# A hybrid encoder step on one Trainium2 core: the modulation of six token tiles made in two halves of the channels

## Chip, core and metric

The kernel runs on one core of one Trainium2 chip. The metric is the device time of one execution in microseconds (us), median over the runs. TensorE (PE in the profile) multiplies; VectorE (DVE), ScalarE (ACT) and GpSimd (POOL) do the rest; SyncE (SP) issues the transfers between HBM and the on-chip memory in one queue.

## What is computed

One layer of a streaming encoder, for a prompt of 2048 tokens and a decode tile of 64 tokens. Its start is what matters here:

```python
mod = jax.nn.silu(c) @ w_ada + b_ada                  # c: (1, 1024), w_ada: (1024, 3072)
shift, scale, gate = jnp.split(mod, 3, axis=-1)
h = _rmsnorm(x, norm_g) * (1.0 + scale[:, None, :]) + shift[:, None, :]
proj = h @ w_in                                       # w_in: (1024, 3080)
u, z_s, q, k, v, z_a, f_logit = jnp.split(proj, IN_SPLITS, axis=-1)
...                                                   # state-space branch on u, attention on q, k, v
y = x + gate[:, None, :] * (mixed @ w_out)
```

u has 512 columns and feeds the state-space branch; f_logit has 8. Everything is float32.

## The kernel before

**Tiles.** The prompt is cut into four groups of 512 tokens, a group into four tiles of 128 tokens (two pairs), the 1024 channels into eight tiles k of 128. Group 3 has the decode tile as well. Pair (g, i) means tiles i and i+1 of group g. float32 products are made as three products of rounded halves: hi x hi, hi x lo, lo x hi, so each weight and each h exists as a `hi` and a `lo` tile (in the profile `whi`, `wlo`, and two tiles that are both named `h`).

**Modulation (class Ada).** The prompt's and the sample's c are transposed and passed through silu into `cT`. `chunk(n)` (n from 0 to 5) loads 512 columns of `w_ada` as two DMAs of 1 MB (tile `wada`, L361), multiplies them with `cT` (eight matmuls per half, four at a time in separate rows of the array), copies the sums to `ms` (ACT, L371), transposes `ms` (four transposes, L127) and reduces them to columns in `mt` (L376). Chunk 0 gives the shift of channel tiles 0 to 3 (`shf`, L388), chunk 1 that of tiles 4 to 7; chunks 2 and 3 give the same for the scale (`gsc`, L390 and L391); 4 and 5 give the gate. A `wada` tile has 16 KB per partition and there are four.

**h (class InProj).** `load(g, i0)` brings in a pair's two x tiles of 0.5 MB (L429), takes the sum of squares (ACT Square, L432), 1/sqrt (`rsq`, L289 on DVE, L290 on POOL) and scales x (DVE, L434). There are four x buffers. `norm(g)` goes through the pairs of a group and, for each two channel tiles, transposes the scaled x (TensorE, L127, two banks), applies scale and shift in the copy out of PSUM (ACT, `hf`, L459) and splits `hf` into hi and lo (DVE, L280 and L284). `put(g)` stores h of groups 0 and 1 to HBM (L469) for the later columns.

**The u columns.** `weights` loads 256 columns of w_in (8 more for f_logit where u's part 0 is meant) as two halves of 0.5 MB (`wst`, L484) and splits each into `whi` (ACT, L282) and `wlo` (DVE, L284). `natural("u", part, groups)` makes, for each token tile, 24 matmuls (8 k, three products; L124, 264 columns in part 0, 256 in part 1) into a PSUM bank, copies it out (L523) and stores it (L538).

**Order.** The program is written as a sequence and a scheduler orders the instructions of each engine; a transfer is issued in the order of the SP queue, and each issue waits for one of eight completion counters, taken in turn. The start is written so: x of pair (0,0); the first w_in weights (u part 0); chunks 0, 2, 1, 3; `params()` (three small loads, L244 to L246); h of groups 0 and 1 and their stores; u parts 0 and 1 of these groups; chunks 4 and 5; `masks()` (a swap matrix and six masks, by selects on POOL and copies on DVE, L252 to L264); then groups 2 and 3.

## Time and profile before

| | us |
|---|---|
| median of three runs | 1456.5 |
| lowest, highest | 1455.73, 1466.12 |
| the profiled execution | 1460.03 |
| its span in the trace | 1458.3 |
| PE busy | 1374.8 (94%) |
| DVE busy | 909.4 (62%) |
| ACT busy | 541.5 (37%) |
| POOL busy | 480.5 (33%) |

The span is the time between the first and the last instruction of the profiled execution. Busy times are sums over the whole span; what bounds the kernel in one stage has to be read from that stage. PE's busy time counts matmuls, PEld the loading of the stationary operand, which runs beside them. A row of a timeline stands for a run of equal instructions: its start, the time from the first to the last of them, and in brackets how long the engine had been idle before and what ended that. The profiled execution is 3.5 us longer than the median run.

### The profile page before, as it was taken

Reading aid. Unit: us, or ns where it says so; the run is one execution under the profiler, and the core shown is the slowest. Engines: PE = TensorE matmul, PEld = TensorE weight load, DVE = VectorE, ACT = ScalarE, POOL = GpSimd, SP = SyncE. Lnnn points to the kernel's source line nnn. Section 1 sums busy time; section 2 is a strip of 40 time slices with the busy share of each in tenths; the row PEclk is TensorE's granted clock in tenths of the full one; section 3 lists DMA queues with packets and bytes.
Section 4 is the critical chain, followed back from the end, with each engine's and each line's share of the span. In section 5 each row is a group of like instructions: output and inputs, shape, how many; then the busy total and the mean of one; then the engine's idle time right before and its main releaser. Section 6 shows DMA issues by size and latency. Waiting matters only on the chain. (4 is left out here: it accounts for less than half of the span.)

```text
span 1458.3 us, 26193 instructions
## 1 busy us (share of the span) xinstructions
PE 1374.8 (94%) x9730; PEld 1082.7 (74%) x9730; DVE 909.4 (62%) x2406; ACT 541.5 (37%) x1156; POOL 480.5 (33%) x452
## 2 busy tenths in 40 slices
PE   5899989999999999999999999999999897999998
PEld 2798889889888889998878855555555454478887
DVE  2646898678767795564214777886886877342331
ACT  3755215343433444333324435445445344300000
POOL 1101356235322362231125413423324527322222
PEclk9999999999999999999999989999999999999999
DMA  9875423323335725235458623133121222054452
GB/s 336 297 274 150 120 65 85 103 81 89 114 88 165 259 77 139 67 98 148 132 169 252 183 93 107 45 98 93 55 74 38 87 63 91 23 159 147 136 150 94
DMA packets 209383, 184.01 MB, mean 126 GB/s; under 512 B 66823, under 2 KB 169955, under 8 KB 208232
## 3 DMA queue, kind: packets, MB, share of 16 engines
q1 hardware_dynamic: 209256, 182.35, 40.8%
q8 instruction: 76, 1.25, 0.4%
q14 instruction: 51, 0.42, 0.1%
HBM read 125.16 MB, written 57.15 MB: 125 GB/s over the span
## 5 line engine op out<-in xcount | busy, mean ns | idle before, releaser
L124 PE MATMUL low<-whi,h 128*128 128x256 f32 (+1 forms) x2112 | 406.9, 289 | 12.7 <-DVE ev L534 7.3
L124 PEld LDWEIGHTS low<-whi,h 128*128 128x128 f32 x2112 | 337.4, 193 | 23.2 <-issue 11.9
L124 PE MATMUL low<-wlo,h 128*128 128x256 f32 (+1 forms) x1088 | 307.9, 286 | 0.6 <-DVE wlo L284 0.6
L1220 DVE CUSTOM_DVE_ANT_0 pb<-twin,cb 128x512 bf16<-128x512 f32 (+3 forms) x328 | 199.7, 609 | 62.8 <-PE twin L124 51.4
L124 PEld LDWEIGHTS low<-wlo,h 128*128 128x128 f32 x1088 | 209.2, 192 | 2.2 <-issue 1.2
L304 ACT ACTIVATE p<-twin 128x1024 f32<-128x1024 f32 (+3 forms) x180 | 150.0, 839 | 146.1 <-PE twin L124 137.4
L124 PE MATMUL low<-h,whi 128*128 128x512 f32 (+1 forms) x640 | 176.7, 362 | 0.0
L124 PE MATMUL bank<-p,vt 128*64 128x512 f32 (+3 forms) x704 | 143.6, 530 | 0.0
L124 PE MATMUL twin<-qs,ks 64*128 64x512 f32 (+3 forms) x1056 | 134.2, 359 | 0.0
L124 PEld LDWEIGHTS low<-h,whi 128*128 128x128 f32 x640 | 115.0, 192 | 17.7 <-issue 1.7
L290 POOL TENSOR_TENSOR qss<-qss,mhalf 128x4 f32<-128x4 f32 (+1 forms) x68 | 77.2, 1137 | 143.0 <-DVE qss L289 118.9
L124 PE MATMUL low<-h,wlo 128*128 128x512 f32 (+1 forms) x320 | 115.4, 361 | 0.0
L284 DVE TENSOR_TENSOR wlo<-wst,whi 128x512 fp32r<-128x512 f32 (+1 forms) x96 | 67.8, 718 | 76.2 <-ACT whi L282 73.5
L1297 DVE TENSOR_TENSOR acc<-acc,p 128x1024 f32<-128x1024 f32 (+4 forms) x89 | 87.5, 983 | 28.7 <-ACT p L304 27.1
L124 PEld LDWEIGHTS twin<-qs,ks 64*128 64x128 f32 x1056 | 95.2, 191 | 10.9
L124 PE MATMUL twin<-sm,kb 64*128 64x512 f32 (+3 forms) x360 | 78.0, 428 | 17.5 <-DVE pm L1220 17.0
L124 PEld LDWEIGHTS bank<-p,vt 128*64 128x64 f32 x704 | 45.4, 141 | 65.6 <-issue 56.2
L175 POOL TENSOR_TENSOR yo<-yo,x 128x512 f32<-128x512 f32 (+1 forms) x34 | 49.0, 1441 | 133.6 <-DVE yo L1531 133.6
L124 PE MATMUL last<-oh,mh 128*128 128x512 f32 (+1 forms) x208 | 81.4, 391 | 0.0
L124 PE MATMUL last<-ol,mh 128*128 128x512 f32 (+1 forms) x208 | 81.1, 390 | 0.0
L124 PE MATMUL last<-oh,ml 128*128 128x512 f32 (+1 forms) x208 | 81.1, 391 | 0.0
L124 PEld LDWEIGHTS twin<-sm,kb 64*128 64x128 f32 x360 | 34.6, 188 | 60.4 <-DVE pm L1220 40.0
(365 smaller groups left out, 2503.8 us busy)
## 6 DMA issues: line engine op xcount, KB each, us to landing
wst<-in_w_in_dram SPq DMA_DIRECT2D x48, 512.0 KB
h<-h SPq DMA_DIRECT2D x16, 1024.0 KB
wada<-in_w_ada_dram SPq DMA_DIRECT2D x12, 1024.0 KB
cb<-cb_d SPq DMA_DIRECT2D x20, 512.0 KB
x<-in_x_prompt_dram SPq DMA_DIRECT2D x16, 512.0 KB
out_dram<-ev SPq DMA_DIRECT2D x64, 128.0 KB
x<-in_x_prompt_dram SPq DMA_DIRECT2D x32, 256.0 KB
out_dram<-yo SPq DMA_DIRECT2D x32, 256.0 KB
```

What stands on the lines that cost most here:

```text
L124: return self.keep(self.pe.matmul(*a, **kw))
L175: PL.tensor_tensor(out, x, y, op=op)
L284: V.tensor_tensor(lo, x, hi, op=ALU.subtract)
L290: PL.tensor_tensor(out, out, bc(mhalf[:out.shape[0]], list(out.shape)), op=ALU.pow)
L304: i = S.activation(out, x, func, **kw)
L1220: V.tensor_tensor_reduce(b[:, :n], ps[:, h, :n], cb[:, h, :n], 1.0, NEG, ALU.add, ALU.max, accum_out=self.pm[:, t, h, pi:pi + 1])
L1297: (PL if j else V).tensor_tensor(y[:rows, :, c0:nq], x[:rows, :, c0:nq], p[:rows, :, :n], op=ALU.add)
```

## The change

A new method `begin` takes the place of the first steps. It makes the h of three pairs, (0,0), (0,2) and (1,0), and multiplies it with u part 1 (columns 256 to 511), in two halves of the channels. Three PSUM banks are held for it, one per pair; each holds the sums of two tiles. For k = 0 to 3, which need chunks 0 and 2 only, each pair is transposed, scaled, split and multiplied (24 matmuls of 256 columns) into its bank; then chunks 1 and 3 are computed, and k = 4 to 7 are added to the same banks. After that the sums are copied out and stored, h of pair (1,2) is made, u part 1 of its two tiles follows, and u part 0 of both groups comes behind that.

The loads of the start have an order of their own, which is pinned on the SP queue: chunks 0 and 2, the first half of w_in's columns (k 0 to 3), x of (0,2), chunk 1, x of (1,0), chunk 3, the second half of w_in's columns. For this `Ada.load` is a method apart from `chunk`, with a tile of 8 KB per partition for each half (four such tiles), `norm` is cut into `normal(g, i0, ks)` and `weights` into `half(k0, c0, n)`. x has six buffers instead of four.

```diff
+    @contextmanager
+    def ordered(*engines):
+        start = len(nc.cur_bb.bb.instructions)
+        yield
+        last = {}
+        for i in nc.cur_bb.bb.instructions[start:]:
+            if not engines or i.engine in engines:
+                if i.engine in last:
+                    tc.add_manual_dep(i, last[i.engine], nosync)
+                last[i.engine] = i.name
...
-        self.wp = Region(e.nc, (R_S5K[0], R_S5U[1] - 4), (18, 36), (54, 72), bufs=4)
+        self.wp = Region(e.nc, (R_S5K[0], R_S5K[0] + 32), bufs=4)
...
+    def load(self, n):
+        for k2 in range(2):
+            w = self.wp.tile([P, 4, 512], F32, name="wada")
+            self.e.nc.sync.dma_start(w, self.e.w_ada[512 * k2:512 * k2 + 512, n * 512:n * 512 + 512]
+                                     .rearrange("(k p) c -> p k c", p=P))
+            self.w[n, k2] = w
...
-        self.xp = Region(e.nc, R_X, (R_S5U[1] - 4, R_S5U[1]))
+        self.xp = Region(e.nc, R_X, (R_S5U[1] - 4, R_S5U[1]), (R_S5K[0] + 32, R_S5K[0] + 40))
...
-            x = self.xp.tile([P, D], F32, tag="x", name="x", bufs=4)
+            x = self.xp.tile([P, D], F32, tag="x", name="x", bufs=6)
...
+    def normal(self, g, i0, ks):
...
+        xs = self.normed[g, i0]
+        c0 = P * i0
+        w = sum(r for _, r in xs)
+        for k in ks:
+            pt = self.pst.tile([P, 2, 256], F32, tag="tr", name="tr")
...
+    def half(self, k0, c0, n):
...
+        st = self.wp.tile([P, 4, 264], F32, tag="wst", name="wst", bufs=2)
+        off = 0
+        for c, w in zip(c0, n):
+            e.nc.sync.dma_start(st[:, :, off:off + w], e.w_in[P * k0:P * k0 + 512, c:c + w].rearrange("(k p) c -> p k c", p=P))
+            off += w
...
+    def begin(self, ad):
+        e = self.e
+        nc, S, PE = e.nc, e.S, e.PE
+        pairs = [(0, 0), (0, 2), (1, 0)]
+        with e.ordered(nc.sync.engine):
+            ad.load(0)
+            ad.load(2)
+            w = [self.half(0, [256], [256])]
+            self.load(0, 2)
+            for n in (0, 2):
+                ad.chunk(n)
+            ad.load(1)
+            self.load(1, 0)
+            ad.load(3)
+            w.append(self.half(4, [256], [256]))
+        banks = [self.ps.hold() for _ in pairs]
+        for n in range(2):
+            if n:
+                for i in (1, 3):
+                    ad.chunk(i)
+            for (g, i0), pm in zip(pairs, banks):
+                self.normal(g, i0, range(4 * n, 4 * n + 4, 2))
+                hi, lo = self.h[g]
+                for j in range(2):
+                    cs = slice(P * (i0 + j), P * (i0 + j + 1))
+                    for k in range(4):
+                        kk = 4 * n + k
+                        for q, (x, y) in enumerate(((hi, 0), (hi, 1), (lo, 0))):
+                            PE.matmul(pm[:, 256 * j:256 * j + 256], x[:, kk, cs], w[n][y][k][:, :256], start=kk == q == j == 0,
+                                      stop=kk == KT - 1 and q == 2, skip_group_check=True)
+        for (g, i0), pm in zip(pairs, banks):
+            del self.normed[g, i0]
+            for j in range(2):
+                t = self.ev.tile([P, 256], F32, tag="ev", name="ev", bufs=4)
+                S.copy(t, pm[:, 256 * j:256 * j + 256])
+                t0 = 512 * g + P * (i0 + j)
+                nc.sync.dma_start(e.u_d[t0:t0 + P, 256:], t)
+            self.ps.free(pm)
+        self.normal(1, 2, range(0, KT, 2))
+        del self.normed[1, 2]
+        self.natural("u", 1, (1,), (w[0][0] + w[1][0], w[0][1] + w[1][1], 256), first=2)
...
         ip.load(0, 0)
         ad = Ada(e)
-        w = ip.weights([0, 3072], [256, 8])
-        for n in (0, 2, 1, 3):
-            ad.chunk(n)
+        ip.begin(ad)
         e.params()
-
         for g in range(2):
-            ip.norm(g)
             ip.put(g)
-        ip.natural("u", 0, (0, 1), w)
-        ip.natural("u", 1, (0, 1))
+        ip.natural("u", 0, (0, 1))
         for n in (4, 5):
+            ad.load(n)
             ad.chunk(n)
         e.masks()
```

The lines named above have other numbers after the change: w_ada is loaded in L371, x in L444, squared in L447 and scaled in L449, w_in is loaded in L512, `ms` copied in L386, `hf` made in L478, h stored in L488, u copied and stored in L558 and L560 for the first six tiles.

The scheduler's order, engine by engine, shows where the steps have gone. First SyncE's queue at the start. `DMAHW0` to `DMAHW7` are the eight completion counters: an issue that waits for one waits for the DMA eight issues before it. Before:

```order
L333 DMA brow_0_163<-in_b_ada_dram 1x1024
L484 DMA wst_0_203<-in_w_in_dram 128x4x256 [waits DMAHW0_49]
L484 DMA wst_0_203<-in_w_in_dram 128x4x8 [waits DMAHW1_49]
L484 DMA wst_1_214<-in_w_in_dram 128x4x256 [waits DMAHW2_49]
L484 DMA wst_1_214<-in_w_in_dram 128x4x8 [waits DMAHW3_49]
L361 DMA wada_0_225<-in_w_ada_dram 128x4x512 [waits DMAHW4_49]
L361 DMA wada_0_225<-in_w_ada_dram 128x4x512 [waits DMAHW5_49]
L361 DMA wada_1_244<-in_w_ada_dram 128x4x512 [waits DMAHW6_49]
```

After, from the first half of w_in's columns on (the four `wada` loads of chunks 0 and 2 stand directly ahead of it, behind `brow`):

```order
L512 DMA wst_0_211<-in_w_in_dram 128x4x256 [waits DMAHW4_49]
L444 DMA x_2_221<-in_x_prompt_dram 128x1024 [waits DMAHW5_49]
L444 DMA x_3_228<-in_x_prompt_dram 128x1024 [waits DMAHW6_49]
L244 DMA bfb_0_107<-in_b_f_dram 128x8 [waits DMAHW7_49]
L245 DMA kg_0_105<-in_k_norm_g_dram 128x64 [waits DMAHW0_49]
L246 DMA qg_0_106<-in_q_norm_g_dram 128x64 [waits DMAHW1_49]
L512 DMA wst_0_211<-in_w_in_dram 128x4x8 [waits DMAHW2_49]
L512 DMA wst_1_286<-in_w_in_dram 128x4x8 [waits DMAHW3_49]
L647 DMA cl_0_1460<-in_cache_logf_dram 128x4x8 [waits DMAHW4_49,DVE_49]
L371 DMA wada_0_203<-in_w_ada_dram 128x4x512 [waits DMAHW5_49,PE_49]
L371 DMA wada_1_205<-in_w_ada_dram 128x4x512 [waits DMAHW6_49,PE_49]
L444 DMA x_4_270<-in_x_prompt_dram 128x1024 [waits DMAHW7_49]
```

The modulation weights of chunks 0 and 2 now stand ahead of w_in; six small loads stand between x_3 and chunk 1, and chunk 1's first load waits for the landing of x_2 (DMAHW5) and for TensorE's use of the buffer.

Second, ScalarE around the copy of chunk 3's sums (`ms_1<-bank_73`). Before:

```order
L371 COPY ms_0_236<-bank_77 128x512
L371 COPY ms_1_255<-bank_73 128x512
L432 ACTIVATE sq_0_143,ss_2_343<-x_2_341 128x1024
L459 ACTIVATE hf_0_311<-low_120,shf_0_112,gsc_0_111 128x256 x2
L459 ACTIVATE hf_1_320<-low_124,shf_0_112,gsc_0_111 128x256 x2
```

After:

```order
L386 COPY ms_0_243<-bank_77 128x512
L478 ACTIVATE hf_0_302<-low_120,shf_0_112,gsc_0_111 128x256 x2
L478 ACTIVATE hf_1_311<-low_124,shf_0_112,gsc_0_111 128x256 x2
L282 CAST whi_2_288<-wst_1_286 128x2x256
L282 CAST whi_3_292<-wst_1_286 128x2x256
L386 COPY ms_1_259<-bank_73 128x512
L282 CAST whi_4_697<-wst_0_211 128x528
```

Between the copies of chunks 1 and 3 there are now scalings of a pair and the two casts of w_in's second half.

Third, VectorE where h of pair (1,2) begins (x_0 and x_1 are its two tiles). Before, the masks stand far behind, among the splits of the decode tile:

```order
L260 MEMSET msk_0_966 128x128
L463 COPY h_16384_1_391<-h_53248_1_392 128x2x64
L264 CAST m_qk_207360_0_93<-msk_0_966 128x128
L256 CAST identw_0_92<-swap_0_957 128x128
L260 MEMSET msk_0_966 128x128
L280 CAST h_16384_1_391<-hf_1_320 128x2x64
```

After:

```order
L449 TENSOR_SCALAR x_0_141<-x_0_141,ss_0_144 128x1024
L260 MEMSET msk_0_970 128x128
L289 TENSOR_SCALAR ss_1_151<-ss_1_151 128x1
L256 CAST identw_0_92<-swap_0_961 128x128
L264 CAST m_qk_207360_0_93<-msk_0_970 128x128
L260 MEMSET msk_0_970 128x128
L449 TENSOR_SCALAR x_1_149<-x_1_149,ss_1_151 128x1024
L264 CAST m_qk_207616_0_94<-msk_0_970 64x128
L260 MEMSET msk_0_970 128x128
L264 CAST m_qk_207616_0_94<-msk_0_970 64x128
L260 MEMSET msk_0_970 128x128
L264 CAST m_kq_207872_0_95<-msk_0_970 128x128
```

Four of the six masks now stand between the scaling of x_0 and the first split of that pair's h, which is two rows further on.

More of the change, by code (lines that the diff above doesn't have):

```diff
@@ L438, in norm @@
     def norm(self, g):
+        for i0 in range(0, len(self.tiles(g)), 2):
+            self.normal(g, i0, range(0, KT, 2))
+            del self.normed[g, i0]
+    def normal(self, g, i0, ks):
         e = self.e
@@ L493, in weights @@
-        return hi, lo, off
-    def natural(self, kind, part, gs, w=None):
+            h, l = self.half(k0, c0, n)
+            hi += h
+            lo += l
+        return hi, lo, sum(n)
+    def half(self, k0, c0, n):
+        e = self.e
+        hi, lo = [], []
+        st = self.wp.tile([P, 4, 264], F32, tag="wst", name="wst", bufs=2)
[3 more added lines that the diff above has]
+            off += w
+        for k in range(0, 4, 2):
+            h = self.wp.tile([P, 2, 264], F32R, tag="whi", name="whi", bufs=5)
+            l = self.wp.tile([P, 2, 264], F32R, tag="wlo", name="wlo", bufs=5)
+            e.split(st[:, k:k + 2, :off], h[:, :, :off], l[:, :, :off], el=self.wlo)
+            hi += [h[:, 0], h[:, 1]]
+            lo += [l[:, 0], l[:, 1]]
+        return hi, lo
@@ L497, in natural @@
+    def natural(self, kind, part, gs, w=None, first=0):
         e = self.e
@@ L505, in natural @@
             ts = self.tiles(g)
-            for i, (t0, r, s) in enumerate(ts):
+            for i, (t0, r, s) in list(enumerate(ts))[first:]:
                 pm = self.ps.tile([P, 512], F32, tag="mm", name="mm")
```

64 lines of the change are left out of this document (21 added, 43 removed).

## Prediction

> **What bounds the kernel now.** I read the busy time by stage first, the stages cut at two events: 39.17 us, when TensorE starts the first matmul that needs the second half of the channels, and 140.59 us, when it starts the first u matmul of token groups 2 and 3. Columns: length, then PE, PEld, DVE, ACT and POOL busy, granted TensorE clock, DMA share, GB/s.
>
> ```profile
> core 0: us, PE busy (x) PEld busy (x) DVE busy (x) ACT busy (x) POOL busy (x), PEclk, DMA share, GB/s
> 0.00:39.17 39.17, 20.95 (x122) 9.16 (x123) 11.73 (x42) 14.51 (x25) 4.68 (x22) 1.00 0.96 327
> 39.17:140.59 101.42, 95.93 (x737) 85.72 (x736) 61.23 (x154) 61.18 (x132) 10.89 (x23) 0.98 0.72 251
> 140.59:1458.30 1317.71, 1257.87 (x8876) 987.77 (x8873) 836.44 (x2212) 465.83 (x1000) 464.95 (x407) 0.98 0.37 111
> 14.90:34.00 19.10, 16.15 (x100) 6.75 (x104) 3.39 (x11) 3.69 (x7) 0.00 (x0) 1.00 1.06 387
> 60.00:70.00 10.00, 8.65 (x71) 8.19 (x70) 6.57 (x15) 8.01 (x17) 1.10 (x2) 1.00 0.92 334
> ```
>
> The last stage holds 1317.71 of 1458.30 us, and the change leaves its instructions as they are. All that can be gained lies in the first two: TensorE is idle there for 18.2 and 5.5 us. In the first the DMA engines are full (0.96; 387 GB/s while the modulation weights stream), so the bound is the order in which bytes come. In the second TensorE is the bound, and its waits are few:
>
> ```profile
> PE low L127 <- ACT hf L459: 6.0, 5, 2.3
> PE low L127 <- DVE x L434: 1.2, 1, 1.2
> PE low L127 <- DVE ss L289: 0.3, 1, 0.3
> ```
>
> That is 7.5 us; the one of 2.3 us ends at the border (it is the wait behind 38.88 below), so 5.2 us belong to the second stage. Last I read the timeline of the start, column by column: start, duration, engine and line, and in brackets what the engine had waited for.
>
> ```profile
> 0.81 0.88 SPq L429 DMA_DIRECT2D x<-in_x_prompt_dram  x2
> 4.39 1.06 ACT L432 ACTIVATE sq<-x 128x1024 bf16<-128x1024 f32 x1 [2.31 <-DMA x<-in_x_prompt_dram]
> 4.39 2.80 SPq L484 DMA_DIRECT2D wst<-in_w_in_dram  x4
> 11.84 1.17 ACT L282 CAST whi<-wst 128x528 fp32r<-128x528 f32 x2 [0.48 <-DMA wst<-in_w_in_dram]
> 14.90 1.94 PE L124 MATMUL bank<-wada,cT 128*32 128x512 f32 x8 [4.36 <-DMA wada<-in_w_ada_dram]
> 17.61 1.93 PE L124 MATMUL bank<-wada,cT 128*32 128x512 f32 x8 [0.77 <-DMA wada<-in_w_ada_dram]
> 23.03 0.20 PEld L124 LDWEIGHTS low<-wada,cT 128*32 128x32 f32 x8 [1.54 <-DMA wada<-in_w_ada_dram]
> 25.84 1.06 PE L124 MATMUL bank<-wada,cT 128*32 128x512 f32 x8
> 28.06 0.39 PE L124 MATMUL low<-whi,h 128*128 128x264 f32 x1
> 33.98 0.30 PEld L124 LDWEIGHTS bank<-wada,cT 128*32 128x32 f32 x8 [0.56 <-DMA wada<-in_w_ada_dram]
> 35.30 0.59 ACT L371 COPY ms<-bank 128x512 f32<-128x512 f32 x1 [4.35 <-PE bank L124]
> 35.94 0.66 PE L127 MATMUL bank<-ident,ms 128*128 128x128 f32 x4 [0.76 <-ACT ms L371]
> 38.88 0.30 PE L127 MATMUL low<-ident,x 128*128 128x128 f32 x1 [2.28 <-ACT hf L459]
> ```
>
> Read it as four facts. The halves of the modulation weights, 1 MB each, land 2.71 us apart (14.90 and 17.61; the fourth at 23.03, the eighth at 33.98). A 0.5 MB tile issued at 0.81 into an idle queue is there at 4.39: 1.36 us for its bytes and 2.2 us of latency. From the landing of the half that completes shift and scale of the first four channel tiles (23.03) to the first h matmul (28.06) pass 5.0 us. From the transposes of the last chunk (35.94) to the first matmul of the second half (39.17) pass 3.2 us.
>
> **The start, term by term.** The 1 MB of w_in that stood ahead goes behind. The first half is then issued when x_0 has landed, at 4.39, lands at 4.39 + 2.2 + 2.7 = 9.3, and the fourth, which completes chunks 0 and 2, at 17.4 where it was 23.03. The scales could be used 5.0 us later, at 22.4, but three things stand ahead of the first h matmul on TensorE and ScalarE: the casts of half the w_in weights, Square of x_2 and x_3, and their transposes. 1.5 MB after 17.4 put x_3 at 21.5. What a landed x tile still needs is seen here:
>
> ```profile
> 59.51 1.06 ACT L432 ACTIVATE sq<-x 128x1024 bf16<-128x1024 f32 x1 [2.59 <-DMA x<-in_x_prompt_dram]
> 62.31 0.87 PE L127 MATMUL low<-ident,x 128*128 128x128 f32 x6 [1.22 <-DVE x L434]
> 42.07 0.29 PE L124 MATMUL low<-whi,h 128*128 128x264 f32 x1
> 42.19 0.28 PE L124 MATMUL low<-wlo,h 128*128 128x264 f32 x1
> 42.31 0.28 PE L124 MATMUL low<-whi,h 128*128 128x264 f32 x1
> 46.90 0.60 PE L127 MATMUL low<-ident,x 128*128 128x128 f32 x4
> 47.25 0.49 PE L124 MATMUL low<-whi,h 128*128 128x264 f32 x2
> ```
>
> 2.8 us from landing to transpose: 24.3, and with the eight transposes 25 us for the first h matmul, 3 us before today's. A matmul takes 0.12 us of the stream (42.07, 42.19, 42.31), a transpose 0.09 (four between 46.90 and 47.25). The first halves of three pairs are 72 matmuls (8.6 us) and 28 transposes (2.5), between them the four halves of chunks 1 and 3 (4 x 1.06) and one set of transposes (0.66): 16.0 us, so TensorE has work until 41.0.
>
> The second half's weights come later than today. Behind 17.4 stand 6.5 MB (half of w_in, x_2 to x_5, chunks 1 and 3), 17.6 us, and about 1 us of gap by six small loads put among them: an issue waits for the landing of the DMA eight before it, so chunk 1's first half can only be issued when x_2 is there. That waiting has a row today,
>
> ```profile
> SPq L484 <- DMA wada<-in_w_ada_dram: 5.1, 3, 2.4
> ```
>
> and gives 36.0 for the last half of chunk 3 (33.98 today). On ScalarE the copy of chunk 3's sums stands behind two casts of w_in's other half, which lands 1.4 us later, 37.4: 1.2 us of casts (the row at 11.84) and 0.6 of copy end at 39.2. The transposes of these sums stand behind the first-half matmuls on TensorE, so they start at 41.0, and the first second-half matmul 3.2 us later at 44.2, which is 5.0 us behind today's 39.17. Until then TensorE has done 48 matmuls (72 for 24) and 19 transposes (36 for 17) more: 5.8 + 1.7 = 7.5 us. **Net gain of the start 2.5 us.** Bounds: 4.1 if the scales follow the copy at 39.2 directly (42.4), and a loss of 0.8 if the small loads cost 4.3 us instead of 1 (their six issues one after the other at the 0.72 us of the row below).
>
> ```profile
> 25.35 0.72 SPq L246 DMA_DIRECT2D qg<-in_q_norm_g_dram  x1
> ```
>
> **Waits of the second stage.** Six buffers for x instead of four mean that the pairs' tiles are there ahead: the 1.22 us at 62.31, where an x tile landed at 59.51, goes. The other 4.0 us wait for hf, a pair's first scaling with two transpose banks; a pair starts in the same manner after the change, so I leave them. **Gain 1.2**, bounds 0 and 5.2.
>
> **The masks.** Today the six masks are built among the h splits of the decode tile:
>
> ```profile
> 130.26 0.29 POOL L261 TENSOR_SCALAR_AFFINE_SELECT msk<-msk 128x128 f32<-128x128 f32 x1
> 137.33 0.29 POOL L261 TENSOR_SCALAR_AFFINE_SELECT msk<-msk 128x128 f32<-128x128 f32 x1 [0.99 <-DVE h L463]
> ```
>
> Six in 7.4 us, one tile, DVE and POOL by turns, 1.2 us each. TensorE then has u matmuls of earlier tiles. Now four and the start of a fifth stand on DVE between the scaling of x_0 of pair (1,2) and its first h split, and behind that split wait its matmuls, behind these all of u part 0. One mask stands before the scaling of x_1 (beside Square, free); three, 3.6 us, behind it, beside the transposes and the scaling into hf, which take some 1.9 us before the split is due (the 3.2 us above less 0.66 of transposes and some 0.7 on DVE). **Loss 1.7** (3.6 - 1.9), bounds 0, if TensorE comes late itself, and 4.9 (four masks with nothing beside them). The copies of u, their stores and the matmuls themselves are the same number as before; 256 columns for 264 in the three pairs is given back in u part 0.
>
> **Sum:** 2.5 + 1.2 - 1.7 = 2.0 us off the profiled execution's 1460.03 us (span 1458.30): 1458.0. That execution lies 3.5 us above the median of the runs, 1456.5, so I forecast **1454.5 us**.
>
> **Rivals.** *Larger gain.* Masks free because chunk 5's weights hold TensorE anyway, all 5.2 us of waits gone, 4.1 at the start: 9.3 us, 1447. For it speaks that TensorE alone bounds the second stage; against it that hf waits come from ScalarE's order. I put its middle at 1449.
>
> *Slower: the queue before pair (1,2).* After 37.4 come half of u part 0's weights, two h stores of 1 MB, chunks 4 and 5 (4 MB) and x_0, x_1: 7.5 MB ahead of the last half of chunk 5, whose matmuls stand before that pair's transposes on TensorE. TensorE is there at 44.2 + 8.6 + 1.1 + 3.2 (72 matmuls, 12 transposes, three halves) + 1.1 for the products with the selector, 58.2. At 2.71 us per MB the load ends at 57.7, so I count no wait. At the 334 GB/s of 60 to 70 us (3.14 us per MB) it ends at 60.9; 2.7 us, of which 1.7 only take the place of the masks' stall. At 251, the mean of the stage (4.18), at 68.7: 10.5 us, less 3.7 (the gain of 2.0 and the masks' 1.7), 6.8 us slower, 1463. From 3.27 us per MB (321 GB/s) the change loses. Against it: the 251 is a mean over a stage in which the queue is often empty. I price it midway between break-even and 251 at 1460.
>
> *Slow matmuls after idling.* The same eight products took 1.94 us at 14.90 and 1.06 at 25.84. If the first pair's 24 matmuls run so after the idle stretches ahead of 25 and 44.2, each costs 24 x 0.12 x 0.83 = 2.4 us: 1459.3. Against it: at 28.06, after little work, matmuls came 0.12 us apart at once, and the granted clock is 1.00 in the whole stretch.
> [...]
>
> *The change does not do what it says.* If x_3's chain or the casts delay the first half by another 2.5 us, the second scales find TensorE no further than the sum needs, and only the mask loss stays against the x wait: 1457.
>
> **How the numbers follow.** Chances: the forecast (1451 to 1458) 0.45, larger gain 0.22, queue 0.15, nothing gained 0.10, slow matmuls 0.08. The bounds of the terms give -9.3 to +5.7 us, 1447 to 1462; with the tails of the two outer rivals outside I give 1447 to 1462. A change under 1% (14.6 us) is about what a measurement of this kernel cannot tell from none. Faster than that needs more than half of the 23.7 us of idle TensorE to vanish, 0.04; slower needs the queue at under 200 GB/s, 0.04; within 1% 0.92.
>
> **What would show it.** Right: chunk 2's last half near 17.4, first h matmul near 25, TensorE dense to 41, a gap there, the second half from about 44; the wait for a scaled x tile (1.22 us) gone; a wait for the split of h beside the masks; group 2's first u matmul some 2 us earlier than 140.59. Wrong: a gap over 5 us between 41 and 50, waits for wada of chunk 5 near 58, matmuls 0.2 us apart after 25, or any shift of more than 3 us in the stage behind 140.59.

## The result, and the profile after

The changed kernel takes 1473.24 us (median of 4 runs, 1471.85 to 1478.14), the kernel before 1457.4 (4 runs, 1455.73 to 1466.12): ratio 1.0102, 95% interval 1.0056 to 1.0149. The forecast was 1454.5 with a range up to 1462; it was wrong in sign. The profiled execution after took 1471.85 us (span 1470.10), 11.8 more than the 1460.03 of the one before.

I read the stages first again. The cuts are 45.14 us (the second half of the channels starts), 91.65 and 102.65 (a hole, below) and 150.60, where as many matmuls are left (8878) as behind 140.31 before. Columns as in the prediction's first fence.

```profile
core 0: us, PE busy (x) PEld busy (x) DVE busy (x) ACT busy (x) POOL busy (x), PEclk, DMA share, GB/s
0.00:45.14 45.14, 28.05 (x185) 17.20 (x185) 18.41 (x56) 21.38 (x39) 6.46 (x25) 0.92 0.98 349
45.14:91.65 46.51, 42.55 (x295) 33.23 (x296) 26.89 (x67) 26.92 (x57) 7.01 (x15) 0.96 0.88 303
91.65:102.65 11.00, 0.32 (x4) 0.09 (x2) 2.60 (x6) 3.03 (x7) 1.10 (x2) 0.59 1.00 303
102.65:150.60 47.95, 47.95 (x373) 46.93 (x373) 25.24 (x67) 25.22 (x57) 1.64 (x3) 0.95 0.41 120
150.60:1470.10 1319.50, 1256.56 (x8878) 986.70 (x8877) 841.91 (x2212) 465.40 (x1000) 459.60 (x407) 0.98 0.37 110
```

Before, up to the same count of matmuls left:

```profile
0.00:140.31 140.31, 116.60 (x854) 94.60 (x855) 72.68 (x194) 75.69 (x156) 15.57 (x45) 0.99 0.79 273
```

Of the 11.8 us, 10.3 (150.60 - 140.31, the same count of matmuls left) are lost before the common point and 1.5 in the long stage behind it (1319.50 for 1317.99). Ahead of that point TensorE was idle for 23.7 us (140.31 - 116.60); now it is idle for 17.1, 4.0 and 10.7 us in the first three stages, 31.7 in all. The difference, 8.0, and 2.3 us more of busy time (118.87 for 116.60) make up the 10.3. One row holds nearly all the idle time that is new: in 91.65 to 102.65 TensorE works 0.32 of 11.00 us while the DMA engines are full (1.00).

What ended that hole is read in the waits between 80 and 110 us (engine, operation and line, who released it; total, times, longest) and in the timelines of ScalarE, VectorE and SyncE there.

```profile
PE low L124 <- DVE lf L596: 10.7, 1, 10.7
ACT whi L282 <- DMA wst<-in_w_in_dram: 6.7, 1, 6.7
DVE wlo L284 <- ACT whi L282: 5.5, 1, 5.5
ACT ev L594 <- DMA u_d<-ev: 2.6, 2, 1.4
```

```profile
100.22 0.63 ACT L282 CAST whi<-wst 128x528 fp32r<-128x528 f32 x1 [6.69 <-DMA wst<-in_w_in_dram]
102.02 0.77 ACT L594 COPY ev<-low 128x256 f32<-128x256 f32 x2 [1.17 <-DMA u_d<-ev]
102.43 0.17 DVE L596 TENSOR_TENSOR lf<-low,bfb 128x8 f32<-128x8 f32 x1 [0.84 <-ACT ev L594]
```

TensorE waits for a PSUM bank of u part 0. The bank is freed by the copy of u (L594) and the add of f_logit behind it (L596). The copy stands on ScalarE behind a cast of w_in for groups 2 and 3, which waits 6.69 us for its load, and then for an `ev` buffer, which a store still reads. Load and stores are late because of SyncE's queue; some of its issues, with start and duration:

```profile
33.56 1.74 SPq L371 DMA_DIRECT2D wada<-in_w_ada_dram  x1
37.20 3.76 SPq L371 DMA_DIRECT2D wada<-in_w_ada_dram  x2
46.17 0.52 SPq L371 DMA_DIRECT2D wada<-in_w_ada_dram  x1
73.76 0.77 SPq L833 DMA_DIRECT2D ba<-in_ssm_b_re_dram  x1
80.04 1.00 SPq L488 DMA_DIRECT2D h<-h  x2
91.40 1.84 SPq L512 DMA_DIRECT2D wst<-in_w_in_dram  x2
95.97 2.38 SPq L560 DMA_DIRECT2D u_d<-ev  x1
98.92 0.52 SPq L560 DMA_DIRECT2D u_d<-ev  x1
```

The four loads of chunks 4 and 5, 4 MB, are issued from 33.56 to 46.69 us. Two of the stores in that list belong to u part 1 of pair (1,0), which ScalarE had copied out at 77.74 and 78.90; their issues come 18 to 20 us later. Before, the same modulation weights came at 100 us and later, in this order of SyncE's queue:

```profile
98.57 0.39 SPq L484 DMA_DIRECT2D wst<-in_w_in_dram  x1
99.70 0.33 SPq L538 DMA_DIRECT2D u_d<-ev  x1
100.08 1.12 SPq L361 DMA_DIRECT2D wada<-in_w_ada_dram  x2
```

The four loads were not alone in coming forward. The 28 small loads of the state-space branch (its parameters and state, 32 KB for the row at 73.76) were first issued at 111.30 us before and are now first issued at 59.44; the `ba` loads and one more hold SyncE from 73.76 to 79.93, and the first two h stores of group 1 stand behind them. From 70 to 80 us the DMA engines moved next to nothing, which the mean of the second stage (303 GB/s) hides:

```profile
70.00:80.00 10.00, 8.58 (x68) 7.80 (x68) 7.30 (x19) 7.52 (x18) 1.61 (x3) 1.00 0.36 62
```

What let the four loads come forward is one pair of lines in the kernel before, which the change leaves out when it cuts `load` from `chunk`:

```diff
         for k2 in range(2):
             x = nc.sync.dma_start(w[:, 4 * k2:4 * k2 + 4], ...)
-            if n > 3:
-                e.tc.keep_in_program_order(x)
```

### The profile page after: what moved, and what is told of

It reads as the page before. It is cut to its first block, busy times and chain, and to the rows that moved or that the text cites. A ratio compares the mean times of both kernels' runs of the same rounds, so it can differ in the third digit from the quotient of the medians.

```text
span 1470.1 us, 26175 instructions
## 1 busy us (share of the span) xinstructions
PE 1375.4 (94%) x9730; PEld 1084.1 (74%) x9730; DVE 915.0 (62%) x2406; ACT 541.9 (37%) x1156; POOL 475.8 (32%) x452
## 5 line engine op out<-in xcount | busy, mean ns | idle before, releaser
L124 PE MATMUL twin<-sm,kb 64*128 64x512 f32 (+3 forms) x360 | 77.9, 428 | 17.3 <-DVE pm L1291 16.9
L282 ACT CAST whi<-wst 128x512 fp32r<-128x512 f32 (+1 forms) x96 | 57.8, 621 | 59.7 <-DMA wst<-in_w_in_dram 35.8
```

What stands on the lines that cost most here:

```text
L124: return self.keep(self.pe.matmul(*a, **kw))
L282: S.copy(hi, x)
```

## The experiments

The theory, Q: the loads of chunks 4 and 5, no longer kept in program order, are moved forward by the scheduler; everything behind them on the one queue comes later, by some 11 us for 4 MB, and TensorE pays where it first needs something from there. Rivals: S, the add of f_logit on VectorE holds the bank; C, TensorE's slow clock behind its idle stretches (granted 0.66 from 20 to 30 and from 45 to 50 us, 0.64 from 100 to 110) costs what the start gains; G, the second half of the channels is gated by the landing of chunk 3, whatever comes ahead; T, TensorE's own work sets the end. Ratios are to the kernel before, run on the same chip, with a 95% interval. "Shift" is by how much later (+) or earlier a profile has the same number of matmuls left as that of before; the kernel after has +3.2 at 81 us, +13.9 at 97 and +10.3 at 149.

**The loads of chunks 4 and 5 kept in order, in the changed kernel.**

```diff
-            self.e.nc.sync.dma_start(w, ...)
+            x = self.e.nc.sync.dma_start(w, ...)
+            if n > 3:
+                self.e.tc.keep_in_program_order(x)
```

> The change with one thing undone: the loads of chunks 4 and 5 of w_ada (4 MB, for the gate) keep their place in the program, as they did before the change, so they are issued behind u part 0 of groups 0 and 1 and not at 37 us. Theory Q (queue): these 4 MB, 2.71 us each, are what brings the first w_in weights of groups 2 and 3 to 99.95 us and makes TensorE stand for 10.95 us ahead of 102.65. Then no wait of TensorE between 80 and 115 us is longer than 3 us, and the time is 11 to 15 us below the changed kernel, 1458 to 1462. Rival S (shape): part 0 with its f_logit add on VectorE, which frees the bank, now comes last and meets the next weights' casts whatever the queue has: a wait of 8 us or more stays there and the time is 1470 or more.

Measured: 1460.68 us, ratio 1.0042 (1.0019 to 1.0065). SyncE's queue, and the stages cut in the same manner:

```profile
73.64 0.83 SPq L562 DMA_DIRECT2D u_d<-ev  x1
74.56 1.03 SPq L446 DMA_DIRECT2D x<-in_x_prompt_dram  x1
75.69 0.79 SPq L562 DMA_DIRECT2D u_d<-ev  x1
```

```profile
0.00:45.14 45.14, 29.41 (x185) 17.56 (x185) 18.41 (x55) 20.92 (x38) 6.46 (x25) 0.89 0.97 350
45.14:139.50 94.36, 89.30 (x669) 79.58 (x670) 54.49 (x139) 55.04 (x121) 9.52 (x20) 0.96 0.70 235
139.50:1458.30 1318.80, 1257.95 (x8877) 988.22 (x8877) 839.38 (x2213) 465.30 (x1000) 458.25 (x407) 0.98 0.37 111
70.00:80.00 10.00, 9.90 (x80) 9.66 (x80) 6.69 (x13) 5.18 (x11) 2.11 (x3) 1.00 1.06 395
```

The last two stores of pair (1,0) are issued at 73.64 and 75.69, some 22 us earlier than in the changed kernel, the 10.7 us of waiting are gone (the longest between 80 and 110 us is 1.4), and the common point is at 139.50, 0.8 us earlier than before. By the ratios 0.6% of the time, some 9 us, come back by an edit to four DMAs. The edit moves more than these four: the small loads go back as well, the first of them to 108.99 us, and from 70 to 80 us the DMA engines move 395 GB/s. So the 22 us are not the 4 MB alone, which take 10.8 us at 2.71 us per MB. An estimate of the rest: the 10.44 us from 69.60 to 80.04, in which the changed kernel moves 65 GB/s instead of such 395, are worth up to 8.7. How much of the loss each of the two makes is not measured apart, and why the scheduler takes the small loads along is not known.

**The same lines taken out of the kernel before.**

```diff
-            if n > 3:
-                e.tc.keep_in_program_order(x)
```

> The kernel before with the one line removed that keeps the loads of chunks 4 and 5 in program order, nothing else. The scheduler then issues them in the first 40 us. Theory Q: the same 4 MB ahead of h stores, x and w_in make this kernel slower than before by 5 us or more (1462 to 1470), with a wait of TensorE of several us where a weight or an x tile comes late between 40 and 110 us. Rival S: within 3 us of before, since the halves are not in it.

Measured: 1470.75 us, ratio 1.0099 (1.0070 to 1.0128). None of the halves is in this kernel, and it loses nearly as much as the whole change. The waits between 20 and 140 us show that its time goes elsewhere (TensorE's two largest):

```profile
PE low L127 <- ACT hf L457: 12.1, 7, 5.1
PE bank L127 <- ACT ms L369: 2.2, 3, 0.8
```

There TensorE waits for the scaling of h (12.1 us for the 6.0 before). The lost pin is the same, the place where it is paid is not. Here too the small loads come forward, from 52.42 us on, and the h stores of group 1 come at 85.7 us and later where they came from 66.0 on before.

**The same loads issued twice in the changed kernel**, 4 MB more (the second copy is the same data).

```diff
+            if n > 3:
+                self.e.nc.sync.dma_start(w, ...)
```

> The change with each load of chunks 4 and 5 issued twice into the same tile (4 MB more in the queue, same values). Theory Q: the wait ahead of the u part 0 matmuls grows by up to 4 x 2.71 = 10.8 us or new waits of that sum appear before it; 1479 to 1485. Rival S: no change beyond 3 us, 1470 to 1476.

Measured: 1478.29 us, ratio 1.0153 (1.0121 to 1.0185). The wait of the bank is 14.6 us for 10.7; the shift at 149 us is +17.1 for +10.3. More bytes ahead, more loss, though 6.8 us of shift for 4 MB are less than the 11 that these take on the queue. The second copies fill the stretch that the small loads had left empty: from 70 to 80 us this kernel moves 398 GB/s, and its first small load comes at 90.2 us. With 8 MB ahead and full DMA engines the last two stores of pair (1,0) come at 98.4 and 99.1, some 24 us later than with the loads in order, where 8 MB take 21.7 and four small loads stand ahead; so here the bytes did it almost alone.

**The h stores of group 1 put behind the first w_in of groups 2 and 3**, in the changed kernel (extra order on SyncE; nothing left out).

```diff
...
+        for x in ip.puts:
+            for w in ip.wst:
+                e.tc.add_manual_dep(x, w, e.nosync)
```

> The change with the 4 MB of the gate left where they are, but the h stores of group 1 (4 MB) tied behind the w_in weights of u part 0 of groups 2 and 3 in the issue queue. Theory Q: those weights land some 10 us earlier, near 90 us, the wait of 10.95 us falls below 3 us, and the time is 1460 to 1465. Rival S: the wait stays at 8 us or more and the time at 1470 or more.

Measured: 1468.84 us, ratio 1.0088 (1.0057 to 1.0119). The bank's wait falls from 10.7 to 4.7 us, but the common point stays where it was (+10.5 us at 149). Up to 150.7 us TensorE is idle for 27.0 us where it was 31.7, and busy for 123.7 where it was 118.9, with the same number of matmuls left: the saved wait has become busy time. From 91.65 us to the common point 382 matmuls take 53.1 us where 377 took 48.3, at a granted clock of 0.69 at first and 0.93 behind 102.65:

```profile
91.65:102.65 11.00, 7.87 (x40) 7.39 (x41) 6.00 (x13) 4.10 (x9) 0.00 (x0) 0.69 1.06 329
```

The time lies between the two expectations. The hole by itself is thus no measure of the loss.

**Filling the idle stretch**, with the loads in order: 60 matmuls of an identity behind chunk 2's transposes, into a bank that nothing reads; and in a second kernel 30 more behind chunk 3's.

```diff
...
+            ad.warm(60)
             ad.load(1)
...
+                ad.warm(30)
             for (g, i0), pm in zip(pairs, banks):
```

> The kernel of e1_gate_late with 60 matmuls of the identity by itself (128x128, into a free bank, never read) put on TensorE between the transposes of chunk 2 and the first h matmul, where it was idle for 4 us. Theory C (clock): after that idle time the first h matmuls of all runs with halves go at half the granted clock (0.50 to 0.63 from 25 to 30 us, 22 to 27 matmuls where 42 fit); with TensorE kept busy the clock there is 1.00, the second half's first matmul comes 1.5 to 2.5 us earlier than the 46 us of e1, and the time is 1 to 3 us below e1. Rival G (gate of the weights): the second half waits for the weights of chunk 3 whatever TensorE does before it; the granted clock may rise, but the second half begins within 0.7 us of e1 and the time is that of e1.

> As e6_warm_first, with 30 more such matmuls behind the transposes of chunk 3, where TensorE was idle for 2 us ahead of the second half. Theory C: granted clock 1.00 from 45 to 50 us as well (0.70 in e1), another 1 to 1.5 us, in all 2.5 to 4.5 us below e1, 1456 to 1458, level with the kernel before. Rival G: no more than 1 us below e1.

Measured: 1456.3 us, ratio 0.9994 (0.9976 to 1.0012) with 60, and 1469.1, ratio 1.0094 (1.0064 to 1.0124) with 90. The stretches of the two, the one with 60 first:

```profile
20.00:35.00 15.00, 15.00 (x72) 15.00 (x71) 6.58 (x17) 7.09 (x14) 2.14 (x4) 0.50 1.03 351
35.00:50.00 15.00, 15.00 (x126) 12.20 (x126) 7.62 (x18) 7.76 (x16) 0.20 (x1) 0.94 0.83 289
```

```profile
20.00:35.00 15.00, 12.90 (x112) 11.23 (x112) 6.57 (x17) 7.81 (x16) 1.79 (x3) 1.00 0.98 340
35.00:45.00 10.00, 7.78 (x42) 4.62 (x43) 5.77 (x11) 5.03 (x11) 0.55 (x1) 0.66 0.97 354
```

Neither says much for C, and the first does not test it, since the clock did not rise. With 60 the granted clock stayed at 0.50, the filling took 13 us and the first h matmul started at 33.30 instead of 24.6; yet at 81 us that kernel is 2.2 us behind the one without filling and no slower over the whole. With 90 the clock was 1.00 from 20 to 35, TensorE was done early, and then stood 4.3 us for chunk 3's weights; the 30 that follow only delay the second half. At 149 us that kernel is 3.6 us behind the one with the loads in order alone; by the ratios it is some 7.5 us slower, and the rest is open. What G says is seen in both: 8.7 us of delay ahead of the first half cost a quarter of that, and a faster first half is waited away.

**The kernel before with chunks 0 and 2 ahead of w_in** on the queue, and nothing else of the change.

```diff
...
-        w = ip.weights([0, 3072], [256, 8])
-        for n in (0, 2, 1, 3):
-            ad.chunk(n)
+        with e.ordered(e.nc.sync.engine):
+            for n in (0, 2):
+                ad.chunk(n)
+            w = ip.weights([0, 3072], [256, 8])
+            for n in (1, 3):
+                ad.chunk(n)
```

> The kernel before with one thing of the change alone: chunks 0 and 2 of w_ada ahead of the first w_in weights in the issue queue, no halves, four x buffers, gate loads in their old place. If the order of the loads by itself brought a gain, this kernel would be 2 us or more faster than before. I expect no gain, 1455 to 1459: the first matmuls can start some 3 us earlier, but chunk 3 lands as late as before and the second half of the first tiles with it.

Measured: 1457.07 us, ratio 1.0006 (0.9985 to 1.0027). The order of the loads by itself is worth nothing that can be measured.

**The changed kernel once more**, on the chip of the last three.

> The changed kernel once more, on the same chip as these runs, to have its distance from e6 to e8 on one chip. Expected as measured before: 1.0 to 1.2 percent above the kernel before; granted clock 0.7 or less from 20 to 30, from 45 to 50 and from 100 to 110 us, and the wait of 10 to 11 us near 92 us in place.

Measured: 1475.42 us, ratio 1.0123 (1.0091 to 1.0154); its wait for the bank is 11.9 us. The loss is there again.

**The transposes of x_2 and x_3 behind the first pair's 24 products**, with the loads in order (`self.tie` is the last of these products).

```diff
...
+                    if (g, i0) == (0, 2) and k < 4:
+                        e.tc.add_manual_dep(y.ins, self.tie, e.nosync)
```

> The kernel of e1_gate_late with one order changed on TensorE: the transposes of x_2 and x_3 stand behind the 24 first-half matmuls of pair (0,0), as they came to stand in e6, but without the 60 filling matmuls. e6 was 7 us faster than e1 by the ratios although its granted clock was 0.50 from 20 to 35 us. Theory O (order): that gain came from the order, work spread so that TensorE had no wait of 2 us ahead of the second half and none behind it; then this kernel is within 2 us of e6, 1455 to 1458, with waits of TensorE below 5 us in sum between 20 and 140. Theory F (filling): it came from the filled stretch; then it is within 2 us of e1, 1459 to 1462, and the waits for hf stay at 7 us.

Measured: 1456.22 us, ratio 1.0002 (0.9978 to 1.0026). The time is the one that theory O names, so the filling is not what made the kernel with 60 matmuls level with the one before. The waits are not: TensorE's waits between 20 and 140 us are 8.9 us in sum, 4.2 of them for the first split of h, and at 149 us this kernel is only 1.2 us ahead of the one with the loads in order alone. How the order would be worth the 0.4% between their ratios is therefore not shown.

**The masks early**, between the scaling of x_0 of pair (1,2) and its first h split, with the loads in order: the place at which the prediction had feared them.

```diff
...
+        self.load(1, 2)
+        e.masks()
+        first = len(e.splits)
         self.normal(1, 2, range(0, KT, 2))
+        e.tc.add_manual_dep(e.splits[first], e.mk[3], e.nosync)
```

> The kernel of e1_gate_late with the masks put where the change had them: between the scaling of x_0 of pair (1,2) and the first h split of that pair on VectorE; the load queue is unchanged. Prediction's term: 1.7 us lost, bounds 0 to 4.9. Read from the trace, TensorE's time at a common later matmul (near 122 us) against e1. Theory Q: the masks are no part of the 11 us, 0 to 2 us against e1. Rival M: masks cost 4 us or more and are a good part of what the change lost.

Measured: 1455.51 us, ratio 0.9986 (0.9967 to 1.0006). At 122 us its profile is 3.2 us behind that of the loads in order alone, at 313 us it is 5.7 ahead. Between 140 and 300 us TensorE's waits for VectorE's `ev` are, in the kernel with the loads in order alone, and here:

```profile
PE low L124 <- DVE ev L607: 8.2, 4, 2.6
```

```profile
PE low L124 <- DVE ev L615: 3.4, 1, 3.4
```

So masks in that place do cost a few us, and the order of the next stage, which comes out otherwise, outweighs it.

**S tested: f_logit copied out by ScalarE**, so that VectorE's add does not hold the bank, in the changed kernel.

```diff
-                        V.tensor_tensor(e.lf[:r, t0 // P], pm[:r, 256:264], e.bfb[:r], op=ALU.add)
+                        f8 = self.ev.tile([P, 8], F32, tag="qss", name="qss", bufs=4)
+                        S.copy(f8[:r], pm[:r, 256:264])
+                        V.tensor_tensor(e.lf[:r, t0 // P], f8[:r], e.bfb[:r], op=ALU.add)
```

> The changed kernel with one op more per tile of u part 0: ScalarE copies the 8 f_logit columns as well, and VectorE adds the bias to that copy, so that VectorE no longer holds the PSUM bank. Theory Q in its exact form: ScalarE's own copies stand behind the cast of w_in weights that land at 100 us, so the bank is held all the same: the wait near 92 us stays at 9 us or more, 1471 to 1477. Rival S: the wait is VectorE's alone and falls below 3 us, 1461 to 1465.

Measured: 1474.63 us, ratio 1.0118 (1.0083 to 1.0153). The wait is now named for ScalarE's copy and is 8.7 us; the shift at 149 us is +9.3. S falls: the add was the last to come, not what it waited for.

**The cast moved behind the copies**: the first late w_in cast on ScalarE waits for u part 0's last copy, in the changed kernel.

```diff
...
+        done, made = e.evs[-1], len(e.casts)
         ip.natural("u", 0, (2, 3))
+        e.tc.add_manual_dep(e.casts[made], done, e.nosync)
```

> The changed kernel with one cast moved: the first cast of the late w_in weights (u part 0 of groups 2 and 3) is tied behind the copies of u part 0 of group 1 on ScalarE, and its wlo follows it on VectorE. The 4 MB of the gate stay early and the weights land as late as before, near 100 us. Theory Q: they are needed only some 20 us later; what stood still was the copies queued behind the cast. The wait of 10.95 us falls below 3 us and the time by 8 to 12 us, 1461 to 1466. If the weights themselves were what TensorE lacked, the wait would only move behind 100 us and the time stay within 3 us of 1473 to 1475.

Measured: 1473.15 us, ratio 1.0104 (1.0077 to 1.0131), no better. The waits between 80 and 110 us of this kernel:

```profile
PE low L124 <- DVE lf L598: 8.5, 1, 8.5
ACT ev L596 <- DMA u_d<-ev: 7.8, 2, 6.3
DVE lf L598 <- ACT ev L596: 5.1, 2, 4.9
```

My reading of the hole, that the cast holds the bank, fell here. With the cast out of the way the copy itself waits, 6.3 us for an `ev` buffer whose store is late on SyncE's queue.

**Buffers of their own for the six early copies**, in the changed kernel: with the cast moved (first), and alone (second). Theory Q2 in these two is Q with both holds in a row.

```diff
-                t = self.ev.tile([P, 256], F32, tag="ev", name="ev", bufs=4)
+                t = ad.sb.tile([P, 256], F32, name="eb", bufs=6)
```

> The changed kernel (six copies still early as in the change) with both holds on the PSUM banks at 92 to 103 us removed: the first late w_in cast stands behind the u-part-0 copies on ScalarE, and the six copies of the u rows of pair (1,0) have SBUF buffers of their own, so that the late copies need not wait for their stores. Theory Q2 (two holds one behind the other, both late because the SP queue is 11 us late: the cast waits for w_in, the shared buffers wait for the u stores): the wait of TensorE ahead of u part 0 of the second group falls from 10.95 us (8.5 with the cast alone moved) to below 3, the second group's common point comes 8 to 10 us earlier than in the change, and the time is 1461 to 1466. Theory T (TensorE's own work is late there too, the late w_in splits are the next to be waited for): the wait moves to the products with w_in and the time stays at 1471 to 1475.

> The changed kernel with own SBUF buffers for the six copies of the u rows of pair (1,0) alone; the cast of the late w_in stays where the change has it. Theory Q2 (two holds in series): the cast by itself still holds the copies until w_in lands near 100 us, so 5 to 9 us of the wait stay and the time is 1468 to 1474. If the stores were the one hold that counts, the wait falls below 3 us and the time is 1461 to 1466, level with the run that removes both. If neither this run nor that one falls, something else holds TensorE there.

Measured: 1470.51 us, ratio 1.0111 (1.0075 to 1.0148) with both, 1467.38, ratio 1.0076 (1.0051 to 1.0102) with the buffers alone. The wait for the bank is gone in both; the waits of the second between 80 and 110 us, and its TensorE in that stretch:

```profile
ACT hf L478 <- PE low L127: 8.8, 1, 8.8
PE low L127 <- ACT hf L478: 4.3, 5, 1.3
ACT hf L478 <- DVE h L284: 3.8, 4, 2.3
```

```profile
92.70:105.20 12.50, 7.99 (x41) 5.37 (x39) 8.23 (x18) 10.62 (x23) 1.12 (x2) 0.76 1.03 313
```

The shift is only about +3.5 us at 97 us, for +13.9 in the changed kernel, but about +10.5 at 109. The scheduler, free of the buffers, has put u part 0's products of groups 0 and 1 first and the transposes of the next pair behind them. So ScalarE stands 8.8 us without work, and then TensorE waits for ScalarE and VectorE, a transpose bank at a time, at a granted clock of 0.76. With the cast alone moved the wait stays, with the buffers alone it goes; but in the second kernel the cast has moved behind the copies too (104.77), so the stores are not shown to be the only hold. Neither kernel gives the 8 to 10 us that were expected. The first comes near the time that theory T names, with the wait at the scaling of h and not at the products with w_in. Because the order on TensorE moved with the buffers, these two don't price the hold by itself.

**The two placements that lost nothing, together**, with the loads in order: masks early, first pair's products first.

> A candidate that would beat both kernels: the change with the late loads of w_ada kept in program order, the row masks of pair (1,2) ahead of the first h split, and the transposes of x tiles 2 and 3 behind the first pair's 24 products. By the two parts' own runs (0.9986 and 1.0002 of the kernel before) it is level with the kernel before or up to 2 us faster: 1453 to 1457. If the two waits were in series and not additive, nothing more than 0.9986 comes.

Measured: 1454.69 us, ratio 0.9978 (0.9948 to 1.0007), the lowest of all the kernels, and its interval still holds 1. Its common point, 135.60 in the profiled execution, is 4.7 us earlier than before:

```profile
0.00:45.14 45.14, 28.27 (x174) 15.96 (x175) 18.15 (x54) 19.98 (x36) 7.25 (x28) 0.89 0.97 342
45.14:135.60 90.46, 87.77 (x683) 77.89 (x682) 53.12 (x140) 54.61 (x121) 10.32 (x17) 1.00 0.75 250
```

TensorE is idle 2.7 us in its second stage, where it was 5.5 before; in the first it is 16.9 for 18.2 (the stages are cut at 45.14 us here, at 39.17 before). That is what the halves have to give here, and it is under what can be told from no change.

## Why the prediction was wrong, by its own steps

**What bounds the kernel: right in the main.** The start is bound by the order of bytes (DMA share 0.98 up to 45.14 us in the changed kernel) and the second stage by TensorE (busy for 89.30 of 94.36 us with the loads in order); the long stage behind the common point grew by only 1.5 us, though it was not left alone: its waits for `ev` in the first 150 us rose from 3.3 to 8.3 us, and the shift is +15.5 at 300 us before it falls back to +11.8 at the end.

**The start: right in its parts.** These rows of the changed kernel's TensorE answer to the forecast's times:

```profile
17.79 1.07 PE L124 MATMUL low<-wada,cT 128*32 128x512 f32 x8 [1.66 <-DMA wada<-in_w_ada_dram]
24.60 0.58 PE L124 MATMUL low<-whi,h 128*128 128x256 f32 x1
39.53 1.06 PE L124 MATMUL bank<-wada,cT 128*32 128x512 f32 x8
45.14 0.66 PE L127 MATMUL low<-ident,x 128*128 128x128 f32 x4 [1.80 <-ACT hf L478]
```

Chunk 2's last half starts at 17.79 (forecast 17.4), the first h matmul at 24.60 (25), the second half with the transposes at 45.14 (44.2). Chunk 3's last half is used at 39.53 where 36.0 was forecast for its landing: its first 15 of 16 completions came from 36.51 to 36.93, the last at 38.38. At 55 us the profile is 2.0 us ahead of before; the forecast had 2.5. (The upper bound of 4.1 is 4.3 by its own terms, 2.5 and 44.2 less 42.4, which changes nothing.)

**The waits of the second stage: wrong, and small.** The wait for a scaled x, 1.22 us before, was to go; between 20 and 92 us the changed kernel has two, 1.6 us in all (0.58 ahead of 64.16 and 0.99 ahead of 66.58).

**The masks: a size off.** I took 1.7 us, for a wait behind the split of h. In the changed kernel that wait does not show (the longest there is 0.25 us); what shows is the 0.99 us for the scaled x_1, whose 1/sqrt stands on GpSimd behind the selects of the swap matrix and of the first mask (64.33 to 65.22). The kernel with the masks early and the loads in order was 3.2 us behind at 122 us, within the bounds of 0 and 4.9.

**The sum without the queue: near at the common point, not in the time.** With the loads in order, the common point came 0.8 us earlier than before, where 2.0 were forecast, and four kernels with that order and other placements (60 fillings, the pair first, the masks early, both of these) measured 0.9978 to 1.0002; the one with 90 fillings measured 1.0094. The plain one measured 1.0042, 1460.68 us where 1454.5 was forecast. Where these 6 us go is open: its profiled execution ends level with that of before, and the 0.8 us that it gains ahead of the common point are lost behind it (1318.80 for 1317.99).

**The rival "the queue before pair (1,2)": the step that failed.** I had seen that 4 MB of chunks 4 and 5 now stand early, and asked one question of them: are they there when TensorE needs them, at 58.2 us? They were: TensorE waits for no modulation weight between 39 and 150 us. "So I count no wait" is where it went wrong. The cost of bytes moved forward is borne by what they are moved past: h stores, x, w_in and the stores of u. I had followed the bytes to their own consumer and to nobody else, and the small loads of the state-space branch that came forward with them are not in that rival's list at all. Against the kernel with the loads in order, the h stores of group 1 come 18 to 22 us later and the last two stores of u 22 to 23; the 4 MB account for 10.8 us of that at the 2.71 us per MB of the prediction, the small loads for up to 8.7 by the estimate above. The hole stands 45 us behind the last issue of these weights, outside the places at which I looked. Against the profiled execution, for which the sum gave 1458.0, a term of the size of the hole, 10.7, makes 1468.7 of 1471.85; that the hole is about as long as 4 MB take is no proof that these alone made it. The medians lie some 5 us further apart, since the profiled execution before is 3.5 us above the median that I took and the one after 1.4 below its own.

**Slow matmuls after idling: there, and given 0.08.** The windows behind the idle stretches of the changed kernel:

```profile
20.00:30.00 10.00, 6.08 (x30) 3.92 (x29) 7.76 (x18) 6.59 (x14) 1.24 (x2) 0.66 1.01 331
45.00:50.00 5.00, 4.86 (x28) 4.72 (x29) 4.30 (x8) 3.65 (x9) 0.00 (x0) 0.66 1.00 395
100.00:110.00 10.00, 7.35 (x43) 7.35 (x44) 5.15 (x14) 5.00 (x11) 0.55 (x1) 0.64 0.80 213
```

The granted clock drops behind 3.9, 1.8 and 10.7 us of waiting, and the first matmuls behind the longest of them come 0.22 us apart (from 103.03 to 104.13) where before they came 0.12 apart (from 42.07 to 42.31). It is a rival beside the forecast and not in place of it: its price, all stretches together, lies in the 2.3 us of additional busy time ahead of the common point, and no run shows it by itself. The prediction held against it that the granted clock was 1.00 in the whole stretch; the trace before has its first record of the clock at 23.72 us, so the column says nothing of the eight products at 14.90, which took 1.94 us where the eight at 25.84 took 1.06.
In the changed kernel's trace the granted clock falls to 0.50 at 21.91, 45.80 and 93.59 us, 1.7, 2.5 and 1.6 us after TensorE's idle time began, and is back at 1.00 at 28.74, 49.22 and 107.24, 4.1 to 4.6 us after work began again. Other profiles show it otherwise: in the kernel filled by 60 matmuls the clock was 0.50 for 15.00 us of 15.00 us busy, and in the changed kernel once more it was 1.00 from 45 to 50 us, though TensorE was idle for 1.8 us between 40 and 50 us there as here.

**The chances.** "Slower by over 1% needs the queue at under 200 GB/s" was worked out from the same one consumer. From 40 to 60 us, while these weights came, the queue moved 407 and 392 GB/s, and the loss came all the same.

## What to carry to other kernels

When a transfer is moved forward, ask what stands behind it on the queue now, and follow that to the first engine that waits, however far: here a store, its buffer, a copy, a PSUM bank and then TensorE, 45 us later. Look also at what else the scheduler moved with it, and at short stretches of the queue: a mean of 303 GB/s hid ten microseconds at 62 GB/s. A line that pins the order of four DMAs can be worth as much as the change it is lost in, so an edit that cuts a function in two is read for the pins that it drops. And when a hole is named for its last releaser, take that away before believing it: behind the add stood the copy, and the copy had both the cast and the buffer ahead of it.

## What the runs showed of the hardware

- In the kernel filled by 60 matmuls TensorE was busy without a gap from 20 to 35 us at half clock: granted 0.50, the identity matmuls of 128 columns 217 ns each (60 in 13.04 us), until the h matmuls had run for some 3 us (33.30 to 36.7; granted 0.83 from 35 to 40 us). With the same 60 matmuls the other kernel had 1.00 over those 15 us. What tells the two apart is open.
- The 16 completions of one DMA lay 1.9 us apart, through a single late one (chunk 3's last half: 15 from 36.51 to 36.93, the last at 38.38).
- One issue held SyncE for 3 us (the h store of 1 MB at 88.23, 3.07 us, with the DMA engines full from 80 to 90, share 1.00), others for 0.3 to 0.4 (the rows at 98.57 and 99.70 before, share 0.54 from 90 to 100). Loads of 32 KB took 0.63 us each, one behind the other from 74.58 on, while the DMA engines stood at a share of 0.36 (70 to 80 us) and moved 62 GB/s: there the bytes were not the bound.
- The same program varies by about 1% from run to run on this chip: the kernel before from 1447.17 to 1464.45 us in 25 runs, the last candidate from 1439.61 to 1457.21 in 12. The mean granted clock goes with the time: 0.984 in the run of 1447.17 us, 0.975 in that of 1464.45, correlation -0.85 over the 25. With so many runs a difference under 0.3% is not told from none.
